# The mixer's output projection as two seven-product units, together with new product orders and PSUM banks around it

## The chip, the cores and the metric

The kernel runs on one core of one Trainium2 chip. The metric is the device time of one execution in microseconds, as the median of several runs. One further execution is recorded by the hardware profiler; its span runs from the first to the last profiled instruction, and its own time is a little longer than the span.

## The reference, cut to what matters

One decoder layer on 512 tokens of width 1024, in float32: a half-step feed-forward, a mixer, a second half-step feed-forward, and a gated embedding at the end.

```python
x = x + 0.5 * swiglu(rmsnorm(x, ffn1_norm), ffn1_wgu, ffn1_wdown)    # 1024 -> 2 x 2816 -> 1024
h = rmsnorm(x, mix_norm)
zq, zk, zv, zc, zg = split(h @ w_in)                  # 1024, 128, 128, 2048, 2048 columns
a = sliding_window_attention(rope(rmsnorm(zq)), rope(rmsnorm(zk)), zv, sinks) @ attn_proj
u = causal_depthwise_conv(ca * sigmoid(cb), dw_w, dw_b)               # ca, cb = split(zc), 31 taps
c = silu(layernorm(u, conv_ln_g, conv_ln_b)) @ conv_proj
merged = sigmoid(ga) * a + sigmoid(gb) * c                            # ga, gb = split(zg)
x = x + merged @ w_out
x = x + 0.5 * swiglu(rmsnorm(x, ffn2_norm), ffn2_wgu, ffn2_wdown)
e = rmsnorm(p @ ple_proj, ple_norm)
x = x + sigmoid(rmsnorm(x, ple_gate_norm) @ ple_gate_w) * e
```

## The kernel before, in words

**Layout.** Activations are held transposed: a tile has 128 channels as partitions and the 512 tokens as its free dimension, so x is eight tiles x0 to x7. Weights come in pieces of 128 x 1024 (512 KB).

**Three products for one.** Every matrix product is made of reduced-precision parts. A weight piece `raw` is split into `whi` (ScalarE copies it into the float32r type) and `wlo` (VectorE subtracts `whi` from `raw`); an activation is split in the same way into `_h` and `_l`. `mm3` then issues three matmuls: low weight times high activation, high times high, high times low. For keys in `SUMMED` (before: `wzc`, `wzg`) the low part of a weight comes without VectorE (`residue`): ScalarE writes -raw and raw in float32r, and an accumulating DMA of GpSimd's queue adds raw to the former.

**Units of seven products.** In the feed-forward steps a product of 2 x 2 blocks is done by `unit` with seven half-size products (256 tokens wide) in place of eight, after Winograd's form of Strassen's method. The sums of weight blocks are made by VectorE in PSUM (tiles `zs`, two banks) and by accumulating DMAs of GpSimd's queue; the sums of activations are the forms 1 to 7 that `act_forms` makes from a pair of results (four half-width differences, and for four tensors a high part on ScalarE and a low part on VectorE). The products run in the order 1, 2, 6, 5, 7, 3, 4, each for two outputs m; after some of them `unit` yields its accumulators b1 and b2 (trace names `wd_a`, `wd_b` for the down projection), which VectorE adds into x. `down` runs two such units (`halves`) over four or three pairs of channel tiles; the last one, of three pairs, finishes x in the order 0, 1, 4, 5 (first unit), then 2, 3, 6, 7.

**The stages around the change.**
- `keys_values` (step K0) follows the first feed-forward. `token_major` computes tokens as partitions; for keys and values, with 256 columns, two token blocks share a bank, so there are two banks and two passes over the eight k-steps. `queries` uses four banks.
- `scores` (steps A0 to A7) makes the attention scores of eight heads for one block of tokens: two groups (jp) of 12 matmuls into two banks each (tiles `sc`), each followed by copies and masking into `s`.
- Then the conv projection (`cp0` to `cp7`): each result is multiplied into `sgb`, added to `mas` and split into `mg`. The output projection `wo0` to `wo7` multiplies `mg` by `wout` with full 512-token products, adds into x, and calls `after`: a split of x times the next norm's gain (`f_h`) and a running sum of squares (`f_ss`).
- The second feed-forward begins with four plain products of 512 tokens (`f_g`, `f_u`), whose k-steps run from 0 to 7; its norm factor is spread by a small product (`f_n_cs`, `f_n_sp`) before `sums` makes its forms.
- At the end the gate `pg0` to `pg7` (`wgate`), each a group of 24 matmuls, is multiplied by the norm factor, passed through the sigmoid, multiplied with the embedding `es` and added to x.

**Order of the work.** Nothing is issued in the order in which it is written. `record` writes the program down, `deadlines` gives each instruction a latest start, and `simulate` is a list scheduler over assumed costs: TensorE takes the first of the next ten groups (`WINDOW`) whose inputs and PSUM banks are there, the other engines take the ready instruction with the earliest latest start. `flex` instructions go to VectorE or GpSimd, whichever takes them first. The order found is what each engine then runs, with real semaphores. There are eight PSUM banks, four slots each for `raw`, `hi` and `lo` weights, and 70 activation tiles. All instructions carry line 1606 in the profile, so they are told apart by tile names.

Of the kernel before, what the change touches and what calls it, by code (L numbers as in the profile page):

```python
# [13 lines left out]
ALU = mybir.AluOpType  # L14
# [389 lines left out]
SUMMED = dict(wzc=0, wzg=0)  # L404
WINDOW = 10
CUT = 4
# [5 lines left out]
def simulate(prog, slots):  # L412
# [159 lines left out]
    while left:  # L572
# [23 lines left out]
        for e in ENGINES:  # L596
# [31 lines left out]
            if hold[e] > t and slack > 10.0 and op.cost > 0.3:  # L628
                continue
            if e == "POOL" and slack > 8.0:  # L630
# [53 lines left out]
def record():  # L684
# [161 lines left out]
    class SumSq:  # L846
# [17 lines left out]

        def in_psum(self, v, last):
# [106 lines left out]
    def unit(name, src, n, col, forms, first=None):  # L972
# [38 lines left out]
        def times(m, f, w, to, start):  # L1011
            with nc.group(f"{name}_p{f}_{m}"):
                for k, x_ in enumerate(forms[f]):
# [12 lines left out]
        w = form(4)  # L1026
        for m in range(2):
            times(m, 4, w, b2, False)
            yield 4, m, b1[m], b2[m]

    def ffn(tag, wgu, wdown, h, gain, ss, after, cuts, wide, plain, mid=None):
# [28 lines left out]
        def gated(i):  # L1060
# [6 lines left out]
            if i % 2:  # L1067
                act_forms(i - 1, us[i - 1][1], u)

        acts = []  # L1070

        def act_forms(i, u0, u1):


            t1, t2 = (ftile(f"{tag}_t{c}{i}") for c in "ab")

            nc.flex.tensor_tensor(t1[:, lo_], u0[:, lo_], u0[:, hi_], op=ALU.subtract)
            nc.flex.tensor_tensor(t2[:, lo_], u1[:, hi_], u0[:, hi_], op=ALU.add)
            nc.flex.tensor_tensor(t1[:, hi_], u1[:, hi_], t1[:, lo_], op=ALU.subtract)
            nc.flex.tensor_tensor(t2[:, hi_], t1[:, hi_], u1[:, lo_], op=ALU.subtract)  # L1080
            one = rtile(f"{tag}_f{i}_1")
            split_into(one[:, lo_], one[:, hi_], u0[:, lo_])
            f = {1: (one[:, lo_], one[:, hi_])}
            for n1, n2, v, sign in ((2, 3, u1, -1.0), (5, 6, t1, None), (7, 4, t2, -1.0)):
                hi, lo = split(f"{tag}_f{i}_{n1}", v, sign)
                f[n1], f[n2] = ((hi[:, t], lo[:, t]) for t in (lo_, hi_))
            acts.append(f)

        def pair(i, T, hn):
# [30 lines left out]
            act_forms(i, u[0], u[1])  # L1120

        def down(p0, p1, halves=(0, 1)):
            np = p1 - p0
            forms = {f: [acts[p][f] for p in range(p0, p1)] for f in range(1, 8)}
            for oo in halves:

                def src(b):
                    return Dram(wdown)[((p0 // 4) * 2 + oo) * 4 + 2 * (b // 10 - 1) + b % 10 - 1][:, 0 : 2 * np * P]

                at = unit(f"{wdown}{p0}_{oo}", src, 2 * np * P, lambda k, m: (m * np + k) * P, forms)  # L1130
                for f, m, b1, b2 in at:
                    o = 2 * oo + m
                    todo = {1: ((b1, 0, lo_), (b2, 0, lo_)), 6: ((b2, 0, hi_), (b1, 1, hi_)),
                            7: ((b2, 1, hi_), (b1, 0, hi_)), 4: ((b2, 1, lo_),)}[f]
                    for b, low, t in todo:
                        v = x[o + 4 * low][:, t]
                        nc.vector.scalar_tensor_tensor(v, b, -0.5 if low else 0.5, v, op0=ALU.mult, op1=ALU.add)
                    if p1 == KF // 2 and f in (7, 4):
                        after(o + (f == 4) * 4)

# [26 lines left out]
    def next_norm(tag, gain):  # L1167
        h, ss = [None] * KD, SumSq(f"{tag}_ss")

        def after(o):  # L1170
            h[o] = split(f"{tag}_h{o}", x[o], gain[:, o : o + 1])
            ss.in_psum(x[o], KD)
# [7 lines left out]
    def proj(tag, key, i, h, nk=KD):  # L1180
# [6 lines left out]
        return ps  # L1187

# [64 lines left out]
    def token_major(tag, key, i0, n_pieces, kper, n):  # L1253

        per = S // n
        banks = [ps_tile(f"{tag}b{b}") for b in range(NT // per)]
        pss = [banks[t % len(banks)][:, (t // len(banks)) * n :][:, 0:n] for t in range(NT)]
        ws = [piece(key, i0 + i) for i in range(n_pieces)]
        with nc.group(tag):
            for t0 in range(0, NT, len(banks)):  # L1260
                for i in range(n_pieces):
                    for kk in range(kper):
                        k = i * kper + kk
                        wk = part(ws[i], slice(kk * n, (kk + 1) * n))
                        for t in range(t0, t0 + len(banks)):
                            xk = part(h2[k], slice(t * P, (t + 1) * P))
                            mm3(pss[t], xk, wk, k == 0, k == KD - 1)
# [9 lines left out]
    def keys_values():  # L1277
        pss = token_major("kv", "wkv", 0, 2, 4, 2 * P)
# [44 lines left out]
    def scores(g, t):  # L1323
# [14 lines left out]
        keys = slice(t0 * W, (t + 1) * W)  # L1338
        for jp in range(2):
            banks = [ps_tile(f"sc{g}_{t}_{jp}{hh}") for hh in range(2)]  # L1340
            bs = [b.rearrange("p (j c k) -> p j c k", j=2, c=2) for b in banks]
            with nc.group(f"sc{g}_{t}_{jp}"):
                for j in range(2):
                    cols = slice((2 * jp + j) * P, (2 * jp + j + 1) * P)
                    for n, (a, b) in enumerate(((1, 0), (0, 0), (0, 1))):
                        for hh in range(2):
                            r = slice(hh * HD, (hh + 1) * HD)
                            nc.tensor.matmul(bs[hh][:, j, 0:nb], qT[a][r, cols], kT[b][r, keys], start=n == 0, stop=n == 2)
            for hh in range(2):
# [135 lines left out]
    def embedding(i):  # L1485
# [7 lines left out]
        for j in range(4):  # L1493
# [7 lines left out]
            nc.scalar.copy(e, ps)  # L1501
            es.append(e)
            sse.add(ps, on_act=True)
        if len(es) == KD:
            rbe = spread("ple", mean_rstd("ple", sse.accs, D))
            for o in range(KD):
                nc.vector.scalar_tensor_tensor(
                    es[o], es[o], g_ple[:, o : o + 1], rbe, op0=ALU.mult, op1=ALU.mult
                )
# [36 lines left out]
    rb4 = None  # L1546
    for o in range(KD):
        ps = proj(f"pg{o}", "wgate", o, h4)
# [3 lines left out]
        n = S // 2 if o == KD - 1 else S  # L1552
        for c in range(0, S, n):
            v = slice(c, c + n)
            nc.vector.tensor_tensor(gt[:, v], ps[:, v], rb4[:, v], op=ALU.mult)
# [55 lines left out]
def _layout(inputs):  # L1611
# [35 lines left out]
    def pairs(w):  # L1647
# [45 lines left out]
        "wout": kxn(f["w_out"][0]),  # L1693
# [25 lines left out]
```

## Time and profile before

| | us |
|---|---|
| median of 3 runs | 1156.57 (1155.35 to 1157.95) |
| the profiled execution's own time | 1154.82 |
| its span | 1153.1 |
| TensorE busy | 1140.8 (99%) |
| VectorE busy | 967.0 (84%) |
| ScalarE busy | 713.5 (62%) |
| GpSimd busy | 398.7 (35%) |

Matmuls overlap: the profile gives a 512-column one 389 ns, but the next one starts 227 ns later, so stages are read by the start times. The granted TensorE clock was 0.999 of full speed. In a timeline row stand the start, the duration, the engine (PE is TensorE, DVE VectorE, ACT ScalarE, POOL GpSimd, SP the queue of SyncE), the operation, the tiles written and read, and in brackets the engine's idle time before it with what ended it.

### The profile page before, as it was taken

Reading aid. Unit: us, or ns where it says so; the run is one execution under the profiler, and the core shown is the slowest. Engines: PE = TensorE matmul, PEld = TensorE weight load, DVE = VectorE, ACT = ScalarE, POOL = GpSimd, SP = SyncE. Lnnn points to the kernel's source line nnn. Section 1 sums busy time; section 2 is a strip of 40 time slices with the busy share of each in tenths; the row PEclk is TensorE's granted clock in tenths of the full one; section 3 lists DMA queues with packets and bytes.
Section 4 is the critical chain, followed back from the end, with each engine's and each line's share of the span. In section 5 each row is a group of like instructions: output and inputs, shape, how many; then the busy total and the mean of one; then the engine's idle time right before and its main releaser. Section 6 shows DMA issues by size and latency. Waiting matters only on the chain.

```text
span 1153.1 us, 19900 instructions
## 1 busy us (share of the span) xinstructions
PE 1140.8 (99%) x7484; PEld 1043.0 (90%) x7484; DVE 967.0 (84%) x1643; ACT 713.5 (62%) x1267; POOL 398.7 (35%) x481
## 2 busy tenths in 40 slices
PE   9999999999999999999999999999999999999998
PEld 7899999999998888878888888888999999999976
DVE  7799978889896799988997865579988788589995
ACT  7655446655366799999984753355654566673541
POOL 1632114222023886875786100035211132251000
PEclk9999999999999999999999999999999999999999
DMA  7456666566547472665654532335666655665421
GB/s 242 125 158 147 183 148 164 142 161 159 134 123 199 109 169 70 147 155 133 150 148 128 128 110 92 99 84 165 147 172 143 158 153 132 151 165 138 128 73 73
DMA packets 52511, 161.55 MB, mean 140 GB/s; under 512 B 6336, under 2 KB 13120, under 8 KB 52416
## 3 DMA queue, kind: packets, MB, share of 16 engines
q1 hardware_dynamic: 39312, 114.12, 30.1%
q0 software_dynamic: 12960, 46.14, 23.5%
q8 instruction: 58, 0.95, 0.3%
q14 instruction: 37, 0.30, 0.1%
q10 hardware_dynamic: 144, 0.03, 0.0%
HBM read 141.40 MB, written 2.10 MB: 124 GB/s over the span
## 4 chain that ended last, share of the span: by engine, by line
PE 94%; ACT 3%; DVE 2%; issue 0%; POOL 0%; DMA 0%; DVEq 0%; POOLq 0%; ACTq 0%
PE wgu_b L1606 17%; PE wgu_a L1606 12%; PE wd_b L1606 10%; PE wd_a L1606 8%; PE f_g L1606 5%; PE f_u L1606 5%; PE gb L1606 4%; PE ap L1606 4%; PE wo L1606 4%; PE cp L1606 4%; PE pg L1606 3%; PE cb L1606 3%; PE ga L1606 3%; PE ca L1606 3%; PE q0b L1606 2%; PE q1b L1606 2%
## 5 line engine op out<-in xcount | busy, mean ns | idle before, releaser
L1606 DVE TENSOR_TENSOR wlo_wgu<-raw_wgu,whi_wgu 128x1024 fp32r<-128x1024 f32 (+1 forms) x141 | 139.8, 1005 | 37.9 <-ACT whi_wgu L1606 37.6
L1606 ACT ACTIVATE whi_wgu<-raw_wgu 128x1024 fp32r<-128x1024 f32 (+1 forms) x141 | 115.4, 838 | 81.1 <-PE wgu_b L1606 32.7
L1606 ACT ACTIVATE whi_wd<-raw_wd 128x1024 fp32r<-128x1024 f32 (+1 forms) x60 | 59.3, 989 | 93.2 <-PE wd_b L1606 62.8
L1606 PE MATMUL wgu_b<-f_t_h,wlo_wgu 128*128 128x256 f32 x408 | 115.5, 283 | 0.0
L1606 PE MATMUL wgu_b<-f_t_l,whi_wgu 128*128 128x256 f32 x408 | 115.5, 283 | 0.0
L1606 PE MATMUL wgu_b<-f_t_h,whi_wgu 128*128 128x256 f32 x408 | 115.5, 283 | 0.0
L1606 POOL TENSOR_TENSOR y<-y,ct 128x511 f32<-128x511 f32 (+27 forms) x90 | 108.4, 1247 | 10.5 <-DVE wlo_wap L1606 5.0
L1606 DVE SCALAR_TENSOR_TENSOR cz<-u,dww,cz 128x510 f32<-128x510 f32 (+28 forms) x145 | 106.5, 735 | 3.3
L1606 POOL DMA_DIRECT2D raw_wgu<-in_wgu x34 | 29.8, 876 | 175.2 <-DMA raw_wgu<-in_wgu 53.3
L1606 PEld LDWEIGHTS wgu_b<-f_t_h,whi_wgu 128*128 128x128 f32 x408 | 78.3, 192 | 0.0
L1606 PEld LDWEIGHTS wgu_b<-f_t_h,wlo_wgu 128*128 128x128 f32 x408 | 78.3, 192 | 0.0
L1606 PEld LDWEIGHTS wgu_b<-f_t_l,whi_wgu 128*128 128x128 f32 x408 | 78.3, 192 | 0.0
L1606 PE MATMUL wgu_a<-f_nl,whi_wgu 128*128 128x256 f32 x272 | 77.0, 283 | 0.0
L1606 PE MATMUL wgu_a<-f_nh,wlo_wgu 128*128 128x256 f32 x272 | 77.0, 283 | 0.0
L1606 PE MATMUL wgu_a<-f_nh,whi_wgu 128*128 128x256 f32 x272 | 77.0, 283 | 0.0
L1606 DVE TENSOR_TENSOR wlo_wd<-raw_wd,whi_wd 128x1024 fp32r<-128x1024 f32 (+1 forms) x60 | 68.5, 1141 | 8.6 <-ACT whi_wd L1606 8.2
L1606 PE MATMUL wd_a<-f_f_h,wlo_wd 128*128 128x256 f32 x264 | 74.7, 283 | 0.0
L1606 PE MATMUL wd_a<-f_f_h,whi_wd 128*128 128x256 f32 x264 | 74.7, 283 | 0.0
L1606 PE MATMUL wd_a<-f_f_l,whi_wd 128*128 128x256 f32 x264 | 74.7, 283 | 0.0
L1606 PE MATMUL wd_b<-f_f_h,wlo_wd 128*128 128x256 f32 x264 | 74.7, 283 | 0.0
L1606 PE MATMUL wd_b<-f_f_h,whi_wd 128*128 128x256 f32 x264 | 74.7, 283 | 0.0
L1606 PE MATMUL wd_b<-f_f_l,whi_wd 128*128 128x256 f32 x264 | 74.7, 283 | 0.0
(505 smaller groups left out, 4041.2 us busy)
## 6 DMA issues: line engine op xcount, KB each, us to landing
raw_wgu<-in_wgu SPq DMA_DIRECT2D x76, 512.0 KB, 4.3
raw_wgu<-in_wgu POOLq DMA_DIRECT2D x34, 512.0 KB, 5.5
raw_wd<-in_wd SPq DMA_DIRECT2D x32, 512.0 KB, 4.5
raw_wd<-in_wd POOLq DMA_DIRECT2D x16, 512.0 KB, 5.5
raw_wzc<-in_wzc SPq DMA_DIRECT2D x16, 512.0 KB, 4.1
wlo_wzc<-raw_wzc POOLq DMA_DIRECT2D x16, 512.0 KB, 5.3
raw_wzg<-in_wzg SPq DMA_DIRECT2D x16, 512.0 KB, 4.6
wlo_wzg<-raw_wzg POOLq DMA_DIRECT2D x16, 512.0 KB, 5.8
```

The source lines that it names most:

```text
L1606: made[op] = getattr(engines[op.eng], op.what)(*a, **k)
```

## The change

- The output projection goes through `unit`: the eight `wo` projections become two units of seven half-size products (`contract`, which `down` now uses too). The conv projection's results are no longer split one by one: result o from 4 to 7 is combined with result o - 4 into a pair's forms by `act_forms`. In the first unit the order of the first two products is changed (`apart`), so that the last pair's second tensor is needed last. The weights are laid out anew on the host side (`_layout`).
- `token_major` gives each token block a bank of its own and makes one pass over the k-steps; keys and values take them in the order `DONE`.
- `scores` issues both of its groups as one (`WHOLE`), with four banks.
- The gate weights `wgate` come by `residue`. Gates 0 and 1 are made side by side in two halves of their k-steps, in the order `DONE` (`proj2`); the last gate is made as two halves of 256 tokens with a PSUM tile each (`halves`).
- The embedding's gain is applied in the ScalarE copy, and its multiplication by the norm factor becomes a `flex` one.
- One constant of the scheduler's rule for GpSimd goes from 4.0 to 1.0 (`KEEP`); `in_sbuf` is added but not used (`INSB` is empty).

```diff
-SUMMED = dict(wzc=0, wzg=0)
+SUMMED = dict(wzc=0, wzg=0, wgate=0)
+KEEP = 10.0, 8.0, 1.0
+WHOLE = True
+INSB = ()
+DONE = 0, 1, 4, 5, 2, 3, 6, 7
...
-                if lock_dve > t and any(o.lock and ls + lag - t < 4.0 for ls, _, o in ready["DVE"]):
+                if lock_dve > t and any(o.lock and ls + lag - t < KEEP[2] for ls, _, o in ready["DVE"]):
...
+            if apart and f1 == 1:
+                for m in range(2):
+                    times(m, 1, w1, b2, True)
+                for m in range(2):
+                    times(m, 2, w2, b1, True, range(len(forms[2]) - 1))
+                for m in range(2):
+                    times(m, 2, w2, b1, True, range(len(forms[2]) - 1, len(forms[2])))
+                    yield f1, m, b1[m], b2[m]
+                continue
...
+    def proj2(tag, key, os, h):
+        out = {}
+        for n in range(2):
+            for o in os:
+                if n == 0:
+                    out[o] = piece(key, o), ps_tile(f"{tag}{o}")
+                w, ps = out[o]
+                with nc.group(f"{tag}{o}_{n}"):
+                    for k in DONE[4 * n : 4 * n + 4]:
+                        mm3(ps, part(w, slice(k * P, (k + 1) * P)), h[k], k == DONE[0], k == DONE[-1])
...
-        per = S // n
-        banks = [ps_tile(f"{tag}b{b}") for b in range(NT // per)]
-        pss = [banks[t % len(banks)][:, (t // len(banks)) * n :][:, 0:n] for t in range(NT)]
+        pss = [ps_tile(f"{tag}b{t}")[:, 0:n] for t in range(NT)]
...
-            for t0 in range(0, NT, len(banks)):
-                for i in range(n_pieces):
-                    for kk in range(kper):
-                        k = i * kper + kk
-                        for t in range(t0, t0 + len(banks)):
+            for k in ks:
+                i, kk = divmod(k, kper)
+                for t in range(NT):
...
-        pss = token_major("kv", "wkv", 0, 2, 4, 2 * P)
+        pss = token_major("kv", "wkv", 0, 2, 4, 2 * P, DONE)
...
-            nc.scalar.copy(e, ps)
+            nc.scalar.activation(e, ps, AF.Copy, scale=g_ple[:, n : n + 1])
...
-                nc.vector.scalar_tensor_tensor(es[o], es[o], g_ple[:, o : o + 1], rbe, op0=ALU.mult, op1=ALU.mult)
+                nc.flex.tensor_tensor(es[o], es[o], rbe, op=ALU.mult)
...
-        nc.vector.tensor_tensor(mas[o], mas[o], sgb[o], op=ALU.add)
-        mg.append(split(f"mg{o}", mas[o]))
+        if o < 4:
+            nc.vector.tensor_tensor(mas[o], mas[o], sgb[o], op=ALU.add)
+        else:
+            nc.vector.scalar_tensor_tensor(mas[o], mas[o], -1.0, sgb[o], op0=ALU.mult, op1=ALU.subtract)
+            mg.append(act_forms(f"mg{o}", mas[o - 4], mas[o]))
...
-    for o in range(KD):
-        ps = proj(f"wo{o}", "wout", o, mg)
-        nc.vector.tensor_tensor(x[o], ps, x[o], op=ALU.add)
-        after(o)
+    contract("wout", "wout", 0, 4, mg, (0, 1), 1.0, after)
...
+    gates = proj2("pg", "wgate", (0, 1), h4)
     for o in range(KD):
-        ps = proj(f"pg{o}", "wgate", o, h4)
+        ps = [gates[o]] if o in gates else halves(f"pg{o}", "wgate", o, h4, 2 if o == KD - 1 else 1)
```

More of the change, by code (lines that the diff above doesn't have):

```diff
@@ L627, in simulate @@
             slack = op.ls + lag - t
[L628 removed]
+            if hold[e] > t and slack > KEEP[0] and op.cost > 0.3:
                 continue
[L630 removed]
+            if e == "POOL" and slack > KEEP[1]:
                 if hold[e] > t:
@@ L863, in add, with in_sbuf @@
             self.n += 1
+        def in_sbuf(self, v, last):
+            n = self.n = self.n + 1
+            to = ftile(f"{self.name}_sq{n}")
+            nc.scalar.activation(to, v, AF.Square)
+            if n == 1:
+                self.accs.append(to)
+            else:
+                nc.flex.tensor_tensor(self.accs[0], self.accs[0], to, op=ALU.add)
         def in_psum(self, v, last):
@@ L970, in record, with unit @@
     lo_, hi_ = slice(0, HS), slice(HS, S)
-    def unit(name, src, n, col, forms, first=None):
+    def unit(name, src, n, col, forms, first=None, apart=False):
         A = {}
@@ L1029, in unit, with act_forms, contract, src @@
             yield 4, m, b1[m], b2[m]
+    def act_forms(name, u0, u1):
+        t1, t2 = (ftile(f"{name}_t{c}") for c in "ab")
+        nc.flex.tensor_tensor(t1[:, lo_], u0[:, lo_], u0[:, hi_], op=ALU.subtract)
+        nc.flex.tensor_tensor(t2[:, lo_], u1[:, hi_], u0[:, hi_], op=ALU.add)
+        nc.flex.tensor_tensor(t1[:, hi_], u1[:, hi_], t1[:, lo_], op=ALU.subtract)
+        nc.flex.tensor_tensor(t2[:, hi_], t1[:, hi_], u1[:, lo_], op=ALU.subtract)
+        one = rtile(f"{name}_1")
+        split_into(one[:, lo_], one[:, hi_], u0[:, lo_])
+        f = {1: (one[:, lo_], one[:, hi_])}
+        for n1, n2, v, sign in ((2, 3, u1, -1.0), (5, 6, t1, None), (7, 4, t2, -1.0)):
+            hi, lo = split(f"{name}_{n1}", v, sign)
+            f[n1], f[n2] = ((hi[:, t], lo[:, t]) for t in (lo_, hi_))
+        return f
+    def contract(name, key, at, np, acts, halves, scale, after):
+        forms = {f: [a[f] for a in acts] for f in range(1, 8)}
+        for oo in halves:
+            def src(b):
+                return Dram(key)[at + 4 * oo + 2 * (b // 10 - 1) + b % 10 - 1][:, 0 : 2 * np * P]
+            steps = unit(f"{name}_{oo}", src, 2 * np * P, lambda k, m: (m * np + k) * P, forms, apart=key == "wout" and not oo)
+            for f, m, b1, b2 in steps:
+                o = 2 * oo + m
+                todo = {1: ((b1, 0, lo_), (b2, 0, lo_)), 6: ((b2, 0, hi_), (b1, 1, hi_)),
+                        7: ((b2, 1, hi_), (b1, 0, hi_)), 4: ((b2, 1, lo_),)}[f]
+                for b, low, t in todo:
+                    v = x[o + 4 * low][:, t]
+                    nc.vector.scalar_tensor_tensor(v, b, -scale if low else scale, v, op0=ALU.mult, op1=ALU.add)
+                if after and f in (7, 4):
+                    after(o + (f == 4) * 4)
     def ffn(tag, wgu, wdown, h, gain, ss, after, cuts, wide, plain, mid=None):
@@ L1067, in gated @@
             if i % 2:
-                act_forms(i - 1, us[i - 1][1], u)
+                acts.append(act_forms(f"{tag}_f{i - 1}", us[i - 1][1], u))
         acts = []
[L1072 to L1087, printed above, removed]
         def pair(i, T, hn):
@@ L1119, in pair @@
                     nc.vector.tensor_tensor(u[1][:, lo_], b2, g[1][:, lo_], op=ALU.mult)
-            act_forms(i, u[0], u[1])
+            acts.append(act_forms(f"{tag}_f{i}", u[0], u[1]))
         def down(p0, p1, halves=(0, 1)):
[L1123 to L1139, printed above, removed]
+            contract(
+                f"{wdown}{p0}", wdown, p0 // 4 * 8, p1 - p0, acts[p0:p1], halves, 0.5,
+                after if p1 == KF // 2 else None,
+            )
         first = None
@@ L1187, in proj, with halves @@
         return ps
+    def halves(tag, key, i, h, cuts):
+        w = piece(key, i)
+        out = []
+        for c in range(cuts):
+            v = slice(c * S // cuts, (c + 1) * S // cuts)
+            out.append(ps_tile(f"{tag}_{c}"))
+            with nc.group(f"{tag}_{c}"):
+                for k in range(KD):
+                    mm3(out[c][:, v], part(w, slice(k * P, (k + 1) * P)), part(h[k], v), k == 0, k == KD - 1)
+        return out
+    def proj2(tag, key, os, h):
[8 more added lines that the diff above has]
+                        mm3(ps, part(w, slice(k * P, (k + 1) * P)), h[k], k == DONE[0], k == DONE[-1])
+        return {o: ps for o, (w, ps) in out.items()}
     us, ys, pas = [None] * KD, [None] * KD, [None] * KD
@@ L1341, in scores @@
             bs = [b.rearrange("p (j c k) -> p j c k", j=2, c=2) for b in banks]
-            with nc.group(f"sc{g}_{t}_{jp}"):
+            bss.append(bs)
+            if not (WHOLE and jp):
+                cm = nc.group(f"sc{g}_{t}_{jp}")
+                cm.__enter__()
+            if 1:
                 for j in range(2):
```

32 lines of the change are left out of this document (17 added, 15 removed).

## The prediction

> **What bounds the kernel now.** I read the page first, then the chain that ended last, the TensorE timeline for its gaps, and the stretches and timelines of the other engines around the places that the diff touches.
>
> ```profile
> span 1153.1 us, 19900 instructions
> ...
> PE 1140.8 (99%) x7484; PEld 1043.0 (90%) x7484; DVE 967.0 (84%) x1643; ACT 713.5 (62%) x1267; POOL 398.7 (35%) x481
> ...
> PE 94%; ACT 3%; DVE 2%; issue 0%; POOL 0%; DMA 0%; DVEq 0%; POOLq 0%; ACTq 0%
> ```
>
> TensorE is busy 99% of the span and carries 94% of the chain. So only two things can move the time: fewer columns streamed, and the few gaps between products. The rest of the diff counts only through those gaps. In the chain's rows the price of a product is its spacing, not its latency:
>
> ```profile
> 73.89 1.44 PE wgu_a L1606 x12
> ...
> 707.23 43.52 PE wo L1606 x192
> ```
>
> A 256-column product costs 1.44/12 = 0.120 us and a 512-column one 43.52/192 = 0.2267 us. Half size is 53% of full size, not 50%. The gaps of TensorE over the whole timeline are these (a bracket is idle time and what ended it; start, duration, instruction):
>
> ```profile
> 346.49 0.28 PE L1606 MATMUL kvb<-wlo_wkv,mix_h_h 128*128 128x256 f32 x1
> 347.95 0.39 PE L1606 MATMUL kvb<-whi_wkv,mix_h_l 128*128 128x256 f32 x1 [1.18 <-DVE mix_h_l L1606]
> ...
> 446.21 0.38 PE L1606 MATMUL sc<-kTh,qT_l 64*128 64x256 f32 x1 [0.58 <-DVE of L1606]
> ...
> 503.35 0.38 PE L1606 MATMUL sc<-kTh,qT_l 64*128 64x256 f32 x1 [1.54 <-DVE s L1606]
> ...
> 1014.36 1.05 PE L1606 MATMUL ple_cs<-ones,ple_sq 128*128 128x1 f32 x8 [0.44 <-POOL ple_sq L1606]
> ...
> 1103.35 0.50 PE L1606 MATMUL pg<-pg_h_l,whi_wgate 128*128 128x512 f32 x1 [0.59 <-DVE pg_h_l L1606]
> ...
> 1104.61 0.50 PE L1606 MATMUL pg<-pg_h_l,whi_wgate 128*128 128x512 f32 x1 [0.30 <-DVE pg_h_l L1606]
> ...
> 1106.55 0.50 PE L1606 MATMUL pg<-pg_h_l,whi_wgate 128*128 128x512 f32 x1 [0.27 <-DVE pg_h_l L1606]
> ```
>
> Lost start to start beyond the normal spacing, the first is 347.95 - 346.49 - 0.12 = 1.34 us: a stall costs its idle time plus some 0.16 for the slow product behind it. With that on each: keys and values 1.34, scores 0.74 + 1.70 = 2.4, embedding 0.60, gate 0.75 + 0.46 + 0.43 = 1.6. In all 6.0 us of stalls to be had, plus what the output projection saves.
>
> **The output projection (wout).** It had 192 products of 512 columns; two units of seven products by 2 outputs by 4 k-steps by 3 passes are 336 of 256. That is 336 x 0.120 = 40.32 against 43.52 us: **-3.20 us**, all on the path since TensorE is dense there. The Trainium skill (TensorE: Matmul & The Clock Gate, Back-to-back issue gap) speaks against it: it gives a sustained 81 ns at 128 and 131 ns at 512 columns, so by a straight line some 98 ns at 256, my estimate from that page; 336 x 98 - 192 x 131 would make this stage 7.8 us longer. The trace does not agree: its two spacings, 120 and 227 ns, are nearly proportional to the columns, so that case gets no chance.
>
> What the units ask of the other engines is the doubtful part:
>
> ```profile
> 685.50:707.00 21.50, 21.50 (x96) 17.80 (x95) 12.48 (x16) 6.79 (x8) 0.00 (x0) 1.00 0.30 96
> 707.00:728.80 21.80, 21.80 (x98) 18.05 (x97) 12.06 (x15) 8.28 (x11) 0.00 (x0) 1.00 0.29 99
> 728.80:750.60 21.80, 21.80 (x98) 18.03 (x97) 12.71 (x16) 8.78 (x12) 0.00 (x0) 1.00 0.30 97
> ...
> 772.40:794.00 21.60, 21.60 (x97) 17.90 (x96) 19.44 (x26) 11.75 (x17) 13.86 (x11) 1.00 0.73 172
> ```
>
> (stretch: length, busy TensorE, weight loads, VectorE, ScalarE, GpSimd, clock, DMA.) In the first three VectorE is busy 57% and GpSimd not at all. Durations for the new work:
>
> ```profile
> 690.95 0.69 DVE L1606 TENSOR_TENSOR sgb<-cp,sgb 128x512 f32<-128x512 f32 x1 [2.29 <-PE cp L1606]
> ...
> 708.60 1.22 DVE L1606 TENSOR_TENSOR wlo_wout<-raw_wout,whi_wout 128x1024 fp32r<-128x1024 f32 x1
> ...
> 708.72 0.64 ACT L1606 ACTIVATE mg_h<-sga 128x512 fp32r<-128x512 f32 x1 [0.34 <-DVE sga L1606]
> ...
> 714.99 0.74 DVE L1606 SCALAR_TENSOR_TENSOR f_h_l<-x,g_all,f_h_h 128x512 fp32r<-128x512 f32 x1
> ...
> 794.47 0.68 DVE L1606 TENSOR_TENSOR zs_wgu<-raw_wgu,zs_wgu 128x512 f32<-128x512 f32 x1
> ...
> 803.16 1.27 DVE L1606 TENSOR_TENSOR wlo_wgu<-zs_wgu,whi_wgu 128x512 fp32r<-128x512 f32 x2
> ...
> 1092.16 0.41 DVE L1606 SCALAR_TENSOR_TENSOR x<-wd_a,x 128x256 f32<-128x256 f32 x1
> ```
>
> From the fifth conv projection's result (691.0) to the new end of wout (750.6 - 3.2 = 747.4) there are 56.4 us. VectorE has in them: the gating of four results, 4 x (0.69 + 0.74) = 5.7; four sets of activation forms, each 4 half-width differences at 0.41, one half low part 0.41 and 3 low parts at 0.74, 4 x 4.3 = 17.1; the weights of two units, each 5 x 1.22 + 2 x 1.27 + 4 x 0.68 = 11.4, so 22.7; 28 updates of x at 0.41 = 11.5; eight norm steps of 0.69 + 0.74 = 11.4; two weights for the next stage, 2.4. Sum 70.8: **14.4 us too much** if nothing moves. Two weights of the first unit (2.4) and the forms that need only the low half's result (4 x 0.82 = 3.3) can be done before 691; the 16 differences (6.6) may go to idle GpSimd. That leaves 2 to 9 us of lateness at the end of wout. How much lateness is free, the end of the first feed-forward shows, where the same tail runs:
>
> ```profile
> 344.45 0.28 PE L1606 MATMUL kvb<-whi_wkv,mix_h_l 128*128 128x256 f32 x1
> ...
> 344.56 0.41 DVE L1606 SCALAR_TENSOR_TENSOR x<-wd_a,x 128x256 f32<-128x256 f32 x1
> 344.89 0.74 DVE L1606 SCALAR_TENSOR_TENSOR x<-wd_b,x 128x256 f32<-128x256 f32 x2
> ...
> 346.15 3.06 DVE L1606 SCALAR_TENSOR_TENSOR mix_h_l<-x,g_all,mix_h_h 128x512 fp32r<-128x512 f32 x3
> ...
> 352.27 0.69 DVE L1606 TENSOR_TENSOR mix_ss_sq<-mix_ss_acc,mix_ss_sq 128x512 f32<-128x512 f32 x1
> ```
>
> VectorE there ended 352.96 - 344.45 = 8.5 us after TensorE had gone on, at the price of the one 1.34 us stall. The second feed-forward asks for its k-steps in the order 0 to 7, each 12 x 0.227 = 2.7 us, so the last two inputs are needed only 16 us in: room for 8.5 us. At the start of wout 24 + 18 products (5.0 us) run before the last result's form 2 is needed, and mult, subtract, split and low part after that result take 0.69 + 0.74 + 0.64 + 0.74 and hand-overs, some 3.2 us: 1.8 us of cover. I take **+0.9 us** of new stalls (ends 0 and 14.4; nearest the feed-forward's row of 1.34, with more cover here). ScalarE has 13 us free in each stretch. SP's queue issues eight loads for wout as before; GpSimd's gets two accumulating DMAs of 512 KB per unit, which the DMA engines at 0.30 have room for.
>
> The differences on GpSimd are not free of charge:
>
> ```profile
> 341.75 2.88 DVE L1606 SCALAR_TENSOR_TENSOR mix_h_l<-x,g_all,mix_h_h 128x512 fp32r<-128x512 f32 x1
> ...
> 340.76 0.87 POOL L1606 DMA_DIRECT2D wlo_wzc<-raw_wzc  x1 [14.07 <-DVE x L1606]
> 341.33 2.74 POOL L1606 TENSOR_TENSOR wlo_wkv<-raw_wkv,whi_wkv 128x1024 fp32r<-128x1024 f32 x1
> ```
>
> Issuing a DMA holds GpSimd 0.87 us, which nothing there waits behind. A 0.74 us instruction of VectorE took 2.88 while GpSimd ran one of 2.74. The Trainium skill (SBUF — State Buffer, Who interferes with whom) says that the two share a port pair and a two-input VectorE instruction is held for the whole of a GpSimd one; the trace agrees. By that rule GpSimd's 6.6 us come back as waits, and the lateness goes to the 9 us end; by the idle column alone it would be 2.
>
> **Keys and values.** Four banks instead of two, all four token blocks per k-step, in the order 0, 1, 4, 5, 2, 3, 6, 7: the products stay the same. The late inputs are those of the second unit of the last down projection. They were wanted 18 products in; now the first four k-steps take 4 x 12 x 0.12 = 5.8 us, to 350.2, and the row above has all low parts done at 349.2. So **-1.3 us**. Against it: four banks must be free at 344.45. The rows at 344.56 and 344.89 are the three reads still to come of the last unit's four banks, and the norm's sum holds one more: four of eight are left, just enough, and a later read would hold the start back. Ends -1.34 and +1.2 (those reads end at 345.6). I take -1.3, since the banks do suffice with the reads where they are.
>
> **Scores.** One block of 24 products with four banks in place of two blocks of 12 with two. Both stalls above are the second block waiting for a bank; now a block starts when all four are free, but asks for more of them at a time. No row shows it: ends -2.4 and +1.7 (the larger of the two again). I take **-1.3**, half.
>
> **Gate.** Outputs 0 and 1 run k-steps 0, 1, 4, 5 first, 5.4 us, then the rest, so the late inputs have cover: up to -1.6. Its weights' low parts go from VectorE to an accumulating DMA of GpSimd:
>
> ```profile
> 1096.98 1.21 DVE L1606 TENSOR_TENSOR wlo_wgate<-raw_wgate,whi_wgate 128x1024 fp32r<-128x1024 f32 x1
> ...
> 1098.25 1.99 ACT L1606 ACTIVATE whi_wgate<-raw_wgate 128x1024 fp32r<-128x1024 f32 x2
> ...
> 1086.12 26.10 SPq L1606 DMA_DIRECT2D raw_wgate<-in_wgate  x7
> ...
> 1100.76 0.40 PE L1606 MATMUL pg<-pg_h_h,wlo_wgate 128*128 128x512 f32 x1
> ...
> wlo_wzg<-raw_wzg POOLq DMA_DIRECT2D x16, 512.0 KB, 5.8
> ```
>
> That takes 8 x 1.21 from VectorE and adds 8 x 1.0 to ScalarE, which idles here. But the second weight, started at 1098.25, would be whole at 1098.25 + 1.0 + 5.8 = 1105.1, and is wanted at 1100.8 + 2.7 = 1103.5: 1.6 us late unless started earlier. Ends -1.6 and +1.6; I take **-1.4**, since raw weights are loaded from 1086 on and a buffer need only be given sooner.
>
> **The rest, at nothing.**
>
> ```profile
> 1149.00 0.75 DVE L1606 TENSOR_TENSOR x<-x,gt 128x256 f32<-128x256 f32 x2
> ```
>
> The last output as two halves: 48 x 0.12 - 24 x 0.2267 = +0.32 on TensorE, and the end has one half instead of two behind it, -0.75/2 (the row's two halves). The embedding's gain moves into a ScalarE copy that runs anyway, and a VectorE pass becomes a plain one of the same length; its 0.60 stall hangs on a GpSimd sum that stays. The planner's smaller hold-back for GpSimd (4.0 to 1.0) reorders work off TensorE; the cover is TensorE's density.
>
> **Sum:** -3.2 - 1.3 - 1.3 - 1.4 + 0.9 = **-6.3 us**. Against the profiled execution's 1154.82 (span 1153.1 and 1.7 around it) that is 1148.5; the median of the runs is 1156.57, 1.75 above, so I forecast 1150.3.
>
> **Rivals.** (A) The sum above, 1150.3, chance 0.42; alone 1148.3 to 1152.3. (B) All stalls go and none comes: -3.2 - 6.0 = 1147.4, chance 0.22. For it: each has a named cause that the diff reorders. (C) Only the product count shows; the order of everything is planned anew and stalls of the old size turn up elsewhere: 1153.4, chance 0.20. (D) VectorE's lateness passes its cover: 14.4 - 8.5 = 5.9 us of stall in place of 0.9: 1155.3, within 0.2% of before (2.3 us, about what a measurement of this kernel can tell from no change), chance 0.10. (E) Slower: VectorE becomes the bound from the fifth conv projection to the next feed-forward, and the whole 14.4 falls on TensorE: 1156.57 - 7.2 + 14.4 = 1163.8. It decides from 9.5 us of stall (7.2 + 2.3). For it: in the feed-forward's stretch from 772.4 VectorE is 90% busy, so lateness isn't made up there; against it: the cover of 8.5. Chance 0.06.
>
> Faster is A, B and C, 0.84; same is D, 0.10; slower is E, 0.06. The range from a little under B to a little over C, 1146.6 to 1154.6, leaves out D and E.
>
> **What would show it.** Right: wout's stage near 40.3 us with no bracket over 1 us; no bracket at the first kvb and pg products; at most one at sc; VectorE over 85% busy from 691 to 750 and its norm sum ending 6 to 10 us after wout. Wrong: brackets on wout or on the next f_g and wgu products that name VectorE (D, E), a wait for wlo_wgate, or a gap ahead of kvb that names x.

## The result

The changed kernel takes **1148.73 us** in the median of four runs (1148.52 to 1148.88); the kernel before, beside it, 1156.99 (1155.35 to 1157.95). The ratio is 0.993, 95% interval 0.9913 to 0.9947: faster by 8.3 us, where 6.3 were forecast. The two profiled executions differ by 1154.82 - 1148.52 = 6.3 us, and their spans by 6.4. So the forecast sum agrees with the difference of the two profiles, in part by luck, as is said below, and the medians differ by 2 us more; that remainder has a cause of its own, found in the experiments below.

The page of the changed kernel:

```profile
span 1146.7 us, 20367 instructions
...
PE 1138.3 (99%) x7652; PEld 1048.8 (91%) x7652; DVE 982.8 (86%) x1677; ACT 729.4 (64%) x1291; POOL 441.0 (38%) x513
```

TensorE still is busy 99% of the span; VectorE, ScalarE and GpSimd all have more to do than before. Where the 6.4 us come from is read from the start of the first product of each stage. The timeline of TensorE before:

```profile
357.29 0.28 PE L1606 MATMUL kvb<-wlo_wkv,mix_h_h 128*128 128x256 f32 x1
...
663.55 0.39 PE L1606 MATMUL cp<-cv_h,wlo_wcp 128*128 128x512 f32 x1
...
707.07 0.39 PE L1606 MATMUL wo<-mg_h,wlo_wout 128*128 128x512 f32 x1
...
750.59 0.39 PE L1606 MATMUL f_g<-f_h_h,wlo_wgu 128*128 128x512 f32 x1
...
1146.99 0.39 PE L1606 MATMUL pg<-pg_h_l,whi_wgate 128*128 128x512 f32 x1
```

and after:

```profile
344.55 0.28 PE L1660 MATMUL kvb<-whi_wkv,mix_h_l 128*128 128x256 f32 x1
...
355.95 0.28 PE L1660 MATMUL kvb<-wlo_wkv,mix_h_h 128*128 128x256 f32 x1
...
661.95 0.39 PE L1660 MATMUL cp<-cv_h,wlo_wcp 128*128 128x512 f32 x1
...
705.47 0.28 PE L1660 MATMUL wout_b<-mg,wlo_wout 128*128 128x256 f32 x1
...
746.20 0.40 PE L1660 MATMUL f_g<-f_h_h,wlo_wgu 128*128 128x512 f32 x1
...
1141.35 0.28 PE L1660 MATMUL pg<-pg_h_l,whi_wgate 128*128 128x256 f32 x1
```

| stage | before | after | difference | forecast |
|---|---|---|---|---|
| to the first kvb | 344.45 | 344.55 | +0.1 | 0 |
| keys and values, first to last product | 12.84 | 11.40 | -1.4 | -1.3 |
| from there to the first cp (queries, scores, the rest of the mixer) | 306.26 | 306.00 | -0.3 | -1.3 |
| conv projection | 43.52 | 43.52 | 0 | 0 |
| output projection, to the first f_g | 43.52 | 40.73 | -2.8 | -2.3 |
| from there to the last pg product | 396.40 | 395.15 | -1.25 | -1.1 |
| last product to the end of the span | 6.13 | 5.39 | -0.7 | -0.4 |

(The forecast's +0.32 for the half-size products stands in the row before the last, its -0.375 in the last.) The output projection in the chain that ended last, and the end of VectorE's norm sum in the timeline:

```profile
705.63 2.87 PE wout_b L1660 x24
708.50 2.53 PE wout_a L1660 x21
711.54 1.70 PE wout_a L1660 x12
713.25 2.88 PE wout_b L1660 x24
```

```profile
711.54 0.39 PE L1660 MATMUL wout_a<-mg_h,wlo_wout 128*128 128x256 f32 x1 [0.16 <-DVE x L1660]
...
748.72 0.68 DVE L1660 TENSOR_TENSOR f_ss_sq<-f_ss_acc,f_ss_sq 128x512 f32<-128x512 f32 x1
```

24 products take 2.87 us, 0.120 each, as forecast. One short wait of 0.16 us names VectorE; VectorE is 19.23 and 20.06 us busy in the two halves of the stage:

```profile
684.00:705.50 21.50, 21.50 (x97) 17.80 (x96) 19.85 (x25) 9.58 (x13) 9.24 (x9) 1.00 0.47 110
705.50:725.60 20.10, 19.94 (x166) 19.74 (x165) 19.23 (x34) 11.17 (x18) 3.85 (x5) 1.00 0.32 93
725.60:746.00 20.40, 20.40 (x173) 20.40 (x172) 20.06 (x34) 12.41 (x18) 0.00 (x0) 1.00 0.45 128
```

(stretch: length, busy TensorE, weight loads, VectorE, ScalarE, GpSimd, clock, DMA share, GB/s.) The norm sum ends at 749.40, 3.2 us after the last product of the projection. The gate's stalls are gone, since the planner put its first half in front of the last unit's last products:

```profile
1095.09 2.75 PE pg L1660 x12
1097.84 2.15 PE wd_b L1660 x18
1099.99 8.20 PE pg L1660 x36
```

### The profile page after: what moved, and what is told of

Its sections match the earlier page's. It is cut to its first block, busy times and chain, and to the rows that moved or that the text cites. A ratio compares the mean times of both kernels' runs of the same rounds, so it can differ in the third digit from the quotient of the medians.

```text
span 1146.7 us, 20367 instructions
## 1 busy us (share of the span) xinstructions
PE 1138.3 (99%) x7652; PEld 1048.8 (91%) x7652; DVE 982.8 (86%) x1677; ACT 729.4 (64%) x1291; POOL 441.0 (38%) x513
## 4 chain that ended last, share of the span: by engine, by line
PE 91%; ACT 4%; DVE 3%; POOL 1%; issue 1%; DMA 0%; POOLq 0%; DVEq 0%; ACTq 0%
PE wgu_b L1660 17%; PE wgu_a L1660 13%; PE wd_b L1660 11%; PE wd_a L1660 8%; PE f_g L1660 5%; PE f_u L1660 5%; PE pg L1660 4%; PE ap L1660 4%; PE cp L1660 4%; PE ga L1660 3%; PE gb L1660 3%; PE cb L1660 2%; PE ca L1660 2%; PE wout_b L1660 2%; PE q0b L1660 2%; PE wout_a L1660 1%
## 5 line engine op out<-in xcount | busy, mean ns | idle before, releaser
L1660 POOL TENSOR_TENSOR y<-y,ct 128x511 f32<-128x511 f32 (+28 forms) x90 | 112.1, 1327 | 9.2 <-DVE wlo_wap L1660 3.8
L1660 DVE SCALAR_TENSOR_TENSOR cz<-u,dww,cz 128x509 f32<-128x509 f32 (+27 forms) x145 | 106.1, 736 | 2.8
L1660 DVE TENSOR_TENSOR wlo_wd<-raw_wd,whi_wd 128x1024 fp32r<-128x1024 f32 (+1 forms) x60 | 73.5, 1225 | 9.7 <-ACT whi_wd L1660 8.9
```

What stands on the lines that cost most here:

```text
L1660: made[op] = getattr(engines[op.eng], op.what)(*a, **k)
```

## The experiments

All were compared with the kernel before on the same chip; its median was 1156.5 to 1156.7 in each comparison.

### What is each part worth: one part undone at a time

**no_wout**: the changed kernel with the output projection as eight full products again.

```diff
-    contract("wout", "wout", 0, 4, mg, (0, 1), 1.0, after)
+    for o in range(KD):
+        ps = proj(f"wo{o}", "wout", o, mg)
+        nc.vector.tensor_tensor(x[o], ps, x[o], op=ALU.add)
+        after(o)
...
```

(The inputs are split one by one again and the weights laid out as before.)

> The changed kernel with the output projection as eight full-width products again, all else kept. Theory (the parts add, each by its own stage): TensorE's stage from the first wout product to the next feed-forward is 43.5 us in place of 40.7, so the time is 2.8 us above the changed kernel's 1148.7, that is 1151.5. Rival (the gain is in how the whole program is ordered anew, not in the product count): the stage is 43.5 us long but the total is within 1 us of 1148.7, or more than 5 us above it, with stalls in other stages.

Measured: 1150.84 us (1150.56 to 1151.39), ratio to before 0.9952 (0.994 to 0.9965). So the units are worth 2.1 us here. Their stage is 43.52 us again, 2.8 more than in the changed kernel; some 0.5 of that comes back further on, where the changed kernel has a wait at the embedding that this one has not (its row stands with the terms below), and 0.3 behind the last product (5.09 us in place of 5.39, with the same last gate). The same two amounts are missing in two_banks, keep4 and scores_two. Each kernel is planned anew, so a part's worth is known to some 0.8 us from the times alone; the stage's own length is the surer figure.

**gate_old**: gate, its weights' low parts and the last output as before.

```diff
-SUMMED = dict(wzc=0, wzg=0, wgate=0)
+SUMMED = dict(wzc=0, wzg=0)
...
-    gates = proj2("pg", "wgate", (0, 1), h4)
-        ps = [gates[o]] if o in gates else halves(f"pg{o}", "wgate", o, h4, 2 if o == KD - 1 else 1)
+        ps = proj(f"pg{o}", "wgate", o, h4)
...
```

> The changed kernel with the gate as it was: one output after another, k-steps 0 to 7, low parts of the weights on VectorE, the last output in one product group. Theory: the stalls ahead of pg products come back, 1.6 us, and the end is 0.4 us longer, so 1150.7. If the spread of the runs before (1155.4 to 1158.0, while the changed kernel's lie within 0.4 us) comes from this stage, its runs spread by 2 us again and the median is 1151.5 to 1153.

Measured: 1150.69 us (1150.51 to 1150.86), ratio 0.9951 (0.9938 to 0.9963): the gate's part is worth 2.0 us, as the theory said. Its runs lie within 0.4 us of each other, so the spread of the kernel before does not come from this stage. Three stalls are back, the largest of them here in TensorE's timeline:

```profile
1099.43 0.39 PE L1660 MATMUL pg<-pg_h_h,whi_wgate 128*128 128x512 f32 x1
1100.68 0.50 PE L1660 MATMUL pg<-pg_h_l,whi_wgate 128*128 128x512 f32 x1 [0.86 <-DVE pg_h_l L1660]
```

**two_banks**: two token blocks share a bank again, two passes, the k-steps still in the new order.

```diff
-        pss = [ps_tile(f"{tag}b{t}")[:, 0:n] for t in range(NT)]
+        banks = [ps_tile(f"{tag}b{b}") for b in range(NT // per)]
+        pss = [banks[t % len(banks)][:, (t // len(banks)) * n :][:, 0:n] for t in range(NT)]
...
```

> The changed kernel with keys and values in two banks and two passes again, but with the new order of k-steps. Theory (order and passes work together): the late k-steps are wanted after 24 products, 2.9 us in, so about 1.3 us of stall returns: 1150.0. Rival (the order of the k-steps alone hides them): within 0.3 us of 1148.7. Second rival (four banks cost something, as a later start or banks missing for the conv products): below 1148.4.

Measured: 1149.59 us (1149.51 to 1149.89), ratio 0.9942 (0.9928 to 0.9955), 0.9 us above the changed kernel. The keys and values take 1.35 us longer, but the wait is a new one:

```profile
347.58 0.39 PE L1663 MATMUL kvb<-wlo_wkv,mix_h_h 128*128 128x256 f32 x1 [1.09 <-POOL wlo_wkv L1663]
```

With two passes a k-step lasts 6 products, and the third of the new order (k = 4) is the first of the second weight piece, whose low part GpSimd has not finished. So this kernel doesn't bring the old stall back, it finds the next input that is late.

**plain_k**: four banks and one pass, but the k-steps in the order 0 to 7.

```diff
-        pss = token_major("kv", "wkv", 0, 2, 4, 2 * P, DONE)
+        pss = token_major("kv", "wkv", 0, 2, 4, 2 * P)
```

> The changed kernel with keys and values in the k-step order 0 to 7, still with four banks in one pass. Theory: the bank for each token block is what counts (each k-step then lasts 12 products, 1.44 us, in place of 6), so less than 0.4 us of the stall returns. Rival: the order counts as much as the banks; then k-steps 2 and 3, the last to be finished, are wanted 2.9 us after the start, and a stall of 1 us or more names mix_h_l, 1149.6 to 1150.

Measured: 1148.98 us (1148.71 to 1149.4), ratio 0.9937 (0.9924 to 0.9951). The stage takes 11.57 us, 0.17 more than with the new order, and no product of it waits 0.25 us. The bank for each block does nearly all, as the theory said; the order, which my working of the prediction rested on as much, does next to nothing.

### The gate: the order or the weights

**gate_vec_low**: the new order of the gate, its weights' low parts on VectorE. **gate_order**: the low parts by DMA, gates 0 and 1 in order, one group each.

```diff
 gate_vec_low:
-SUMMED = dict(wzc=0, wzg=0, wgate=0)
+SUMMED = dict(wzc=0, wzg=0)
 gate_order:
-    gates = proj2("pg", "wgate", (0, 1), h4)
...
```

> The changed kernel with the low parts of the gate's weights on VectorE as before; the new order of gates 0 and 1 is kept. Theory: the order of the k-steps is what removes the three stalls at the gate (1.6 us), so this stays within 0.3 us of the changed kernel. Rival: the 9.7 us taken from VectorE are what lets its last inputs come in time; then 1 to 1.6 us more, 1149.7 to 1150.4.

> The changed kernel with gates 0 and 1 each as one group in k-step order 0 to 7, as before; the weights' low parts still come by the accumulating DMA. Theory: the stalls for the last low parts of the activations return at the gate, 1 to 1.6 us, 1149.7 to 1150.4. Rival: with 9.7 us less on VectorE the low parts come in time in any order, and it stays within 0.3 us of the changed kernel.

Measured: 1150.02 us (1149.85 to 1150.34; ratio 0.9946, 0.9933 to 0.9958) and 1150.13 us (1150.04 to 1150.64; ratio 0.9947, 0.9934 to 0.9959). Each half alone leaves 1.3 to 1.4 of the 2.0 us on the table: for gate_vec_low my theory (the order alone does it) is wrong and the rival right, for gate_order the theory holds in size but not in place. In gate_vec_low the stall is at the gate:

```profile
1098.82 1.22 DVE L1660 TENSOR_TENSOR wlo_wgate<-raw_wgate,whi_wgate 128x1024 fp32r<-128x1024 f32 x1
...
1101.35 0.50 PE L1660 MATMUL pg<-pg_h_l,whi_wgate 128*128 128x512 f32 x1 [1.33 <-DVE pg_h_l L1660]
```

VectorE makes a weight's low part just ahead of the low parts of the inputs that are waited for. In gate_order it is ahead of the gate, in the last unit of the down projection:

```profile
1095.45 0.95 DVE L1659 TENSOR_TENSOR wlo_wd<-raw_wd,whi_wd 128x768 fp32r<-128x768 f32 x1
...
1096.46 0.39 PE L1659 MATMUL wd_b<-f_f_h,wlo_wd 128*128 128x256 f32 x1 [1.28 <-DVE wlo_wd L1659]
```

A unit's weight is late there, and in the changed kernel the gate's first 12 products (2.75 us at 1095.09) run in exactly that place. So the half-group is filler for a late weight as much as cover for late inputs.

### The units and VectorE

**wout_alone**: the kernel before with nothing but the output projection as two units.

> The kernel before with only the output projection changed to two units of seven half-size products. Theory: before less 2.8 us (1156.99 to 1154.2), with the stalls of keys and values (1.3 us), scores (2.4 us) and gate (1.6 us) still in the trace. Rival (VectorE late after the output projection): the stage is 40.7 us but the next feed-forward shows stalls on f_g or wgu products, and the time is within 1 us of before.

Measured: 1155.7 us (1154.02 to 1156.39), ratio 0.9991 (0.9983 to 1.0). The units alone gain 0.8 us (the interval reaches to no gain), not the 2.1 they are worth in the changed kernel: the rival's time, but not its place, since the stalls are in the projection itself. The projection's stage takes 42.90 us and has two stalls:

```profile
715.39 0.38 PE L1663 MATMUL wout_a<-mg_l,whi_wout 128*128 128x256 f32 x1 [1.28 <-DVE mg_l L1663]
...
716.92 0.38 PE L1663 MATMUL wout_a<-mg_h,wlo_wout 128*128 128x256 f32 x1 [0.80 <-DVE x L1663]
```

The first is the last pair's form 2: the 1.8 us of cover that the prediction counted there were not enough. So VectorE's lateness is real. What the changed kernel has against it is the scheduler's constant:

**keep4**, the changed kernel with the constant as before, and **wout_keep1**, wout_alone with the new one.

```diff
 keep4:
-KEEP = 10.0, 8.0, 1.0
+KEEP = 10.0, 8.0, 4.0
 wout_keep1:
-KEEP = 10.0, 8.0, 4.0
+KEEP = 10.0, 8.0, 1.0
```

> The changed kernel with the scheduler's hold-back for GpSimd at 4.0 as before. Theory: GpSimd takes fewer of the half-width differences and sums, VectorE falls behind in the output projection, and two stalls of about 1.4 and 1.0 us that name VectorE return there (42.5 to 43 us for its stage in place of 40.7), for some 2 us more in all, 1150.5 to 1151. Rival: the constant only reorders work off TensorE, and the time stays at 1148.5 to 1149.

> The kernel before with the output projection as two units and the scheduler's hold-back at 1.0, nothing else changed. Theory: the stalls of 1.44 and 0.96 us that the same units had at 4.0 go, the stage takes near 40.7 us, and the median is some 2 us below that of the units at 4.0, 1153 to 1154.5. Rival: the stalls came from the order around the projection (scores, gate), not from the constant, and the stage keeps 42 to 43 us.

Measured: keep4 1150.2 us (1150.02 to 1151.78), ratio 0.9953 (0.994 to 0.9967); wout_keep1 1153.26 (1151.54 to 1153.69), ratio 0.9973 (0.9964 to 0.9982). The constant decides both ways: 42.90 us for the stage and the same two stalls in keep4, 40.73 and none over 0.2 us in wout_keep1. But not for the reason that the theory gave. GpSimd makes the same differences in both. What changes is the order of ScalarE and VectorE; keep4:

```profile
707.58 0.68 DVE L1660 SCALAR_TENSOR_TENSOR sga<-sga,sgb 128x512 f32<-128x512 f32 x1
...
709.59 0.61 ACT L1660 ACTIVATE mg_h<-sga 128x512 fp32r<-128x512 f32 x1
...
709.72 1.84 DVE L1660 TENSOR_TENSOR wlo_wout<-raw_wout,whi_wout 128x1024 fp32r<-128x1024 f32 x1 [0.26 <-ACT whi_wout L1660]
711.48 0.68 DVE L1660 SCALAR_TENSOR_TENSOR mg_l<-sga,mg_h 128x512 fp32r<-128x512 f32 x1
```

and after:

```profile
706.88 0.69 DVE L1660 SCALAR_TENSOR_TENSOR sga<-sga,sgb 128x512 f32<-128x512 f32 x1
...
707.60 0.63 ACT L1660 ACTIVATE mg_h<-sga 128x512 fp32r<-128x512 f32 x1 [0.26 <-DVE sga L1660]
...
708.68 0.95 DVE L1660 SCALAR_TENSOR_TENSOR mg_l<-sga,mg_h 128x512 fp32r<-128x512 f32 x1
```

After, the last pair's low part starts 1.8 us after its input (`sga`) did, and ends at 709.63. In keep4 it starts 3.9 us after its input did and ends at 712.16, 2.5 us later. Three things make this up: `sga` itself starts 0.7 us later; ScalarE copies a full weight (708.63 to 709.69) ahead of the high part, which the low part needs, so that is there at 710.20 in place of 708.23; and VectorE then makes that weight's low part, 1.84 us, ahead of the input's. wout_alone and wout_keep1 differ in the same way. Why the planner's rule for GpSimd turns these orders round was not traced.

**load2**: two more VectorE instructions of 0.74 us for each input of the second feed-forward.

```diff
             h[o] = split(f"{tag}_h{o}", x[o], gain[:, o : o + 1])
+            for _ in range(2 if tag == "f2" else 0):
+                nc.vector.scalar_tensor_tensor(
+                    h[o][1], x[o], gain[:, o : o + 1], h[o][0].bitcast(F32), op0=ALU.mult, op1=ALU.subtract
+                )
```

> The changed kernel with the low part of each of the eight inputs of the second feed-forward computed three times in place of once, two more VectorE instructions of 0.74 us each, 16 x 0.74 = 11.8 us of VectorE work in the output projection's stage and just behind it. Theory: VectorE's lateness is the price of the units and has a cover; in the changed kernel its norm sum ended 3.2 us after TensorE had left the projection, and some 8.5 us are free, so 5.3 us of the 11.8 are hidden and some 4 to 8 us show up as stalls that name VectorE at the projection's or the next products, 1152.5 to 1157. Rival: the planner moves the work elsewhere and VectorE still has room, under 1 us, 1149 to 1149.7.

Measured: 1150.7 us (1150.44 to 1151.08), ratio 0.9951 (0.9939 to 0.9964): 2.0 us for 11.8 us of work, between the theory's 4 to 8 and the rival's 1. There is not one more stall in the output projection nor at the feed-forward's first products. All 24 low parts of this input, from one view of the tile:

```profile
L1664 DVE SCALAR_TENSOR_TENSOR f_h_l<-x,g_all,f_h_h x24: 740/744/748, 728.1 to 765.6; 128x512 fp32r<-128x512 f32 x24
```

The last starts 19 us after TensorE left the projection at 746.72. What is lost comes 77 us later, in the sums of the feed-forward:

```profile
823.62 0.28 PE L1664 MATMUL wgu_b<-f_t_l,whi_wgu 128*128 128x256 f32 x1
825.08 0.39 PE L1664 MATMUL wgu_b<-f_t_h,wlo_wgu 128*128 128x256 f32 x1 [1.18 <-ACT f_gs L1664]
```

This is one stall of 1.34 us; another 0.5 lies in small ones between 800 and 850. It names ScalarE, and VectorE was idle from 821.2 to 823.0, just before, so whether this is the lateness carried on or only another order of the work isn't shown. At the projection and the next products VectorE's lateness had room for 11.8 us more, and rival E, the 14.4 us on TensorE, was far away.

### The scores, and why the medians differ by more than the profiles

The kernel before spreads over 2 us or more from run to run, the changed one over 0.4. wout_alone spread too, and its trace showed a granted clock of 0.57 from 505 to 508 us, behind the stall in the scores. So:

**scores_alone**: the kernel before with its two groups of scores as one. **scores_two**: the changed kernel with two groups.

```diff
 scores_alone, against before:
-            with nc.group(f"sc{g}_{t}_{jp}"):
+            if not (WHOLE and jp):
+                cm = nc.group(f"sc{g}_{t}_{jp}")
+                cm.__enter__()
...
 scores_two, against after:
-WHOLE = True
+WHOLE = False
```

> The kernel before with one part of the change: the scores of a token block as one group of 24 products in four banks. Theory: the two stalls in the scores (0.74 and 1.70 us before) shrink to a few tenths, and with them goes what made the kernel before spread over 2 us from run to run (a halved TensorE clock for some 2 us behind the longer stall). Then the runs lie within 1 us of each other and the median is 2.5 to 4 us below that of the kernel before, near 1153. Rival: the stalls are worth only their bracket, 1 to 1.5 us, and the spread of 2 us has another origin and stays.

> The changed kernel with the scores in two groups of 12 products and two banks, as before. Theory: the stalls of some 0.7 and 1.7 us return and the spread of the runs with them, 1150.5 to 1153 us with a median 2.5 to 4 us above the changed kernel, and in a slow run a stretch of some 2 us behind the stall has a granted clock near 0.5. Rival: 1 to 1.5 us above it, with runs as close together as those of the changed kernel.

Measured: scores_alone 1154.02 us (1153.75 to 1154.5 in 11 runs), ratio 0.9981 (0.9972 to 0.999). The spread is gone and 2.7 us of the median with it, within the theory's 2.5 to 4. scores_two 1148.52 us in the median (1148.36 to 1149.85), ratio 0.9937 (0.9925 to 0.9949): four of its five runs are as short as the changed kernel's and one, the profiled one, is 1.4 us longer. So the theory's median was wrong, and what the stall costs had to be taken apart. In that execution of scores_two:

```profile
499.00:502.00 3.00, 1.21 (x21) 1.01 (x17) 2.22 (x6) 3.00 (x7) 3.00 (x4) 1.00 0.58 179
...
503.50:507.00 3.50, 3.50 (x16) 2.73 (x13) 3.42 (x11) 3.48 (x9) 3.50 (x4) 0.51 0.57 115
```

and, with the product that ended the stall, products of 512 columns in it:

```profile
502.34 0.38 PE L1660 MATMUL sc<-kTh,qT_l 64*128 64x256 f32 x1 [2.13 <-DVE s L1660]
...
505.31 0.63 PE L1660 MATMUL gb<-mix_h_l,whi_wzg 128*128 128x512 f32 x1
505.74 0.63 PE L1660 MATMUL gb<-mix_h_h,wlo_wzg 128*128 128x512 f32 x1
```

The same stretch of the profiled execution before, with its stall of 1.54 us in the same place:

```profile
503.50:507.00 3.50, 3.50 (x32) 3.03 (x33) 3.50 (x10) 3.47 (x8) 3.17 (x4) 1.00 0.88 187
```

Behind the stall the clock is halved in one execution and full in the other: the products start 0.43 us apart in place of 0.227. From the product that ended the stall to the eighth `gb` product it is 4.87 us in scores_two and 3.33 before: 1.5 us lost to the clock alone.

Over all runs the two cases can be counted by the spans. The 44 runs of the kernel before beside these experiments fall into two groups with nothing between: 17 with a span of 1153.2 to 1153.6 us and a mean clock of 0.999, and 27 with 1154.7 to 1155.6 and 0.997 or 0.998. The profiled execution (1153.1) is of the first group. wout_alone (4 at 1152.3 to 1152.6, 7 at 1153.7 to 1154.6) and wout_keep1 (2 and 8) split in the same way; every kernel with the scores in one group is tight, but for one run of keep4 (1149.8 beside 1148.2 to 1148.7). Its two stalls of 1.28 and 0.80 us lie within 3 us of each other and may do the same, but that run left no trace. So the kernel before pays 1.7 us for a halved clock in six runs of ten, and one group of scores takes away the stall that leads to it. That the second group's runs have the halved clock in this very place is shown by three profiles (wout_alone, wout_keep1, scores_two), none of the kernel before itself.

Without the clock, the stall's removal is worth little in the changed kernel. scores_two's four other runs have spans of 1146.7 to 1147.0, the changed kernel's are 1146.7 to 1147.1. Its stage from keys to conv projection took 319.30 us, 1.54 of it the clock, so 317.76 against 317.40; and the changed kernel loses 0.5 at the embedding, where scores_two doesn't. Beside the kernel before, by the first group's median of 1153.3, scores_alone's 1152.2 is 1.1 us.

## Why the prediction was right, and where it was off

**The sum.** Forecast -6.3; between the profiles -6.3, and against the first group of the kernel before (17 runs, median 1155.1) 1148.73 - 1155.1 = -6.4. The likeliest case, A, is what came, but in part by luck: the scores were taken 1.0 us too high, and the output projection (0.5), the gate and the end (0.5 together) too low, so the errors cancel.

**The step that failed: the 1.75 us** between the profiled execution and the median, which I carried over as if it were a constant of the measurement. It is the halved clock behind a stall that the change removes. The forecast time is 1.6 us too high for this alone. The sign was there to see: three runs from 1155.35 to 1157.95, and a profiled one below them all.

**Output projection, -3.2 and +0.9.** The spacing of 0.120 us held, 336 of them are 40.32 of the 40.73 us; the new stalls are 0.4, half of what I took. But this depends on the scheduler's constant, which I costed at nothing ("reorders work off TensorE"): with the old value they are 2.6 (42.90 - 40.32), and keep4 is 1.5 us longer in all. That is the second mis-sized term, hidden because the change brings its own remedy. The 1.8 us of cover at the start was mis-sized too: the four steps behind the conv projection's last result took 4.0 us in the changed kernel (705.67 to 709.63), not 3.2, and the 42 products ahead end at 710.5, which leaves 0.9. VectorE came out at 19.2 and 20.1 us busy in the stage's halves, over 85% as forecast; its norm sum ended 3.2 us after TensorE had left, not 6 to 10. GpSimd was 9.2 us busy from 684 to 705.5, mostly with the differences; a VectorE instruction beside one took 0.95 us in place of 0.68 (`mg_l` in the rows above), so they were not free, but the lateness came near the lower end of the 2 to 9 us. Rival D was true of the units alone in kind (2.6 us of stall, not 5.9), rival E wasn't.

**Keys and values, -1.3:** measured -1.4. The reason was half right, since the order does 0.2 of it and the banks the rest. Four banks were free at the start, so the worry about a later start came to +0.1.

**Scores, -1.3:** measured -0.3 in the profiles. Both stalls are gone, but small losses of 0.25 to 0.6 us took their place; the largest has this row:

```profile
462.37 0.50 PE L1660 MATMUL q1b<-whi_wq,mix_h_l 128*128 128x512 f32 x1 [0.41 <-DVE of L1660]
```

That is rival C's mechanism, in this stage and, with 0.5 us, at the embedding. The part's worth over many runs is larger than its stall, through the clock.

**Gate, -1.4:** undoing it costs 2.0 us: three stalls of together 1.7, and 0.6 for the longer end, less 0.3 for the half-size products. So the stalls were worth the full 1.6 to 1.7, and the shorter end 0.6 to 0.7 in place of 0.375. The late second weight that I feared was not: its accumulating DMA was issued at 1095.16, where I had reckoned with 1099.3.

```profile
1090.94 0.86 POOL L1660 DMA_DIRECT2D wlo_wgate<-raw_wgate  x1 [10.12 <-DVE x L1660]
1095.16 0.86 POOL L1660 DMA_DIRECT2D wlo_wgate<-raw_wgate  x1 [3.36 <-ACT wlo_wgate L1660]
```

**The embedding, 0:** its old stall stayed as forecast, and another came beside it:

```profile
1004.18 0.39 PE L1660 MATMUL wgu_b<-f_nh,wlo_wgu 128*128 128x256 f32 x1 [0.36 <-ACT es L1660]
1007.76 1.05 PE L1660 MATMUL ple_cs<-ones,ple_sq 128*128 128x1 f32 x8 [0.45 <-POOL ple_sq L1660]
```

## What to carry to other kernels

Where runs of one kernel fall into two groups, the gap between the profiled execution and the median is a cost with a place in the trace, and a change may remove it: look for the longest stall of TensorE and the granted clock behind it before carrying the gap over. When work is moved to engines that seem free, what decides is the order in which the busiest of them takes it: here one weight ahead of one input, on ScalarE and VectorE, was 2 us of the stage, and a single constant of the planner chose between them. Removing one stall tends to bring the next late input to light (a weight piece in two_banks, a unit's weight in gate_order), so a part's worth is measured with the other parts in place.

## What the runs showed of the hardware that I had not expected

A gap of TensorE of 1.5 to 2.1 us can be enough for a halved clock. The stalls in the scores (brackets 1.53 in wout_alone, 2.13 in scores_two, 2.11 in wout_keep1) were followed, 0.7 to 1.2 us after TensorE had resumed, by 3.4 us at a granted clock of 0.50, and whether it happens changes from run to run of the same program. The stall of 1.34 us at the keys did not show it in any of the traces that have it. What decides seems to be where the stall falls. wout_alone, with its stall from 501.9 to 503.4, and then the kernel before, with one of the same length from 501.8 to 503.35:

```profile
500.74:504.15 3.41, 1.88 (x29) 1.60 (x27) 1.94 (x6) 3.41 (x8) 3.13 (x4) 1.00 0.62 179
504.15:507.56 3.41, 3.41 (x20) 2.81 (x18) 3.41 (x10) 3.38 (x8) 3.08 (x4) 0.50 0.77 147
...
498.90:502.31 3.41, 2.90 (x30) 2.18 (x28) 2.47 (x6) 3.41 (x6) 2.79 (x4) 1.00 0.59 184
502.31:505.72 3.41, 2.37 (x26) 2.15 (x27) 2.87 (x10) 3.38 (x8) 3.41 (x4) 1.00 0.90 239
```

In the three traces with a halved stretch (from 503.50, 504.15 and 505.32) the clock falls again behind the last product (at 1145.20, 1152.68 and 1150.44), 188, 190 and 189 times 3.4133 us later. Counted back in such steps from the same fall in the kernel before (1150.84), one step ends at 502.31, inside its stall: TensorE is busy 2.90 and 2.37 us on the two sides, against 1.28 to 1.88 us in the step ahead of each halving. No threshold follows: no_wout has a step with 1.83 us busy near its end and full clock behind it. The Trainium skill (TensorE: Matmul & The Clock Gate, What's actually happening) describes a window of 3.4 us that runs free of the kernel, which fits the length, the steps and the chance; it asks for at least one idle window before the clock falls, and here a gap of about half a window was enough.
